# First layer of a two-layer diffusion trunk: row dot products write partial sums, the sink becomes a softmax column, the gate exponentials take their offset as a bias

## The chip, the cores and the metric

The kernel runs on one core of a Trainium2 chip. The metric is device time in microseconds (us) of one execution. Three runs of the kernel before gave 2087.85, 2090.25 and 2090.61 us, median 2090.25. One further execution was recorded by the profiler.

## The reference, cut to what matters

Two layers over 640 tokens (128 context, 512 latent) of width 2048, all in fp32. Every layer first makes its modulation vectors (shift, scale, gate) from a conditioning vector, one set for the context tokens and one for the latent ones:

```
shift, scale, gate = split(silu(cond) @ ada_w[l] + ada_b[l], 3)
h = rms_norm(x, norm_g[l]) * (1 + scale) + shift
y = mixer(h @ w_in) * silu(h @ w_gate);  x = x + gate * (y @ w_out[l])
```

Layer 0 mixes with window attention (8 heads, a sink logit per head that enters the softmax denominator and nothing else) and with gated linear attention (GLA, 4 heads, forward and backward). Of the softmax: `p = softmax([scores, sink])`, then the sink's column is dropped. Of GLA, with `b` the running sum of the log gates inside a 128-token chunk, the elementwise part is

```
Qp = q * exp(b/16)             KS = k * exp((b[end] - b)/16)
QI = q * exp((b - b[mid])/16)  KI = k * exp((b[mid] - b)/16)
```

for both directions and each of five chunks. Layer 1 has neighbourhood attention and a spatial-gating MLP; the change is not about it.

## The kernel before, in words

**The matrix work.** Every projection is `chunk` by `chunk`: 128 output columns, 16 input blocks k of 128 rows, the 640 tokens in two halves of 320 (322 where two shift columns ride along). To keep fp32 accuracy each operand is split into a high and a low part in a format TensorE takes at full speed, and three products are added: `acth*whi`, `actl*whi`, `acth*wlo` (method `mm_k`, issued from `mm`, line 400). Four blocks k make a unit of weights: ScalarE (ACT) rounds the raw weights into `whi`, GpSimd (POOL) subtracts into `wlo`. A unit feeds 24 matmuls. The split weights live in a ring of `RING = 2560` columns (line 39), five units of 512 columns.

**Who fixes the order.** The program is one list per engine, written out when it is built. A planner (`Pace`, with fixed costs by engine and size) keeps a clock for every engine; small jobs are Python generators that are advanced between matmuls (`tick`) and that wait (`until`) till the planner holds their inputs for ready. So what the generators issue, and between which matmuls, follows from the planner's costs, while on the chip each engine runs its list in order and waits on semaphores. All vector, scalar and pool instructions are recorded by one helper, so they all carry line 215; TensorE's matmuls carry line 400, its transposes line 405, and a group of small matmuls at the start line 1432.

**PSUM.** Eight banks. In layer 0 after the start, three serve the projections (`npj = 3`, line 2628), three the small matmuls (`sm`), and banks 6 and 7 (printed bank_73 and bank_74) hold two rows of the conditioning vector, repeated on all partitions.

**The start** (`start`, up to about 150 us) makes layer 0's scale by small matmuls (line 1432) and half of its shift by dot products, and runs the first six chunks in windows as the activations come in. The dot products (`shifts`, line 1455; for later vectors `ada_task`, line 1269) take a row block of 512 weights per instruction: DVE multiplies by the conditioning row and reduces; the sum over the four blocks q of a row is made by passing the accumulator on, as the scalar that the next reduction starts from. Each reduction is two instructions, the product (`CUSTOM_DVE_ANT_0` in the profile, `ISA` in a listing) and a read of the accumulator. When POOL is free by the planner, a dot product for the latent tokens goes there instead (`offload`): POOL multiplies into `prod`, ACT copies `prod` with an accumulator output into a column of `psum`, and four adds fold the four blocks into the result. At the end of the start the shift `sh` is folded, the shift columns of the activations are written, and TensorE transposes `sh` (line 405) before the first chunk that uses shift columns, the 96-wide `w_rb`.

**GLA** (four heads, about 150 to 500 us): for each head the chunks k, q and two of v are projected. The evacuation of a chunk (`lin`) is: DVE multiplies a bank by `rstd`; ACT copies two bias columns of the same bank to `bc`; ACT adds the bias in two pieces. `gla_dir` does the elementwise part for one direction: DVE subtracts `b` from its chunk ends into KS and from its middles into KI over all 640 columns, ACT takes four exponentials of 640 columns, DVE multiplies by q or k. `tok_major` transposes a finished v chunk (five transposes in two small banks, two copies by ACT), and `gla_pe` then begins with the transposes of KS.

**Attention** (to about 830 us) works on pieces of 128 to 512 scores: `soft1` masks and takes the row maximum on DVE, ACT exponentiates with `-max` as bias and an accumulator output `den`; ACT also makes `es = exp(sink - max)`; `soft2` adds `es` to `den` on ACT, DVE takes the reciprocal, ACT scales the piece.

## Time and profile before

| | |
|---|---|
| runs | 2087.85, 2090.25, 2090.61 us; median 2090.25 |
| the profiled execution | 2094.82 us, of which the span from first to last instruction is 2093.0 us |
| granted TensorE clock | 0.996 over the span |
| PE busy | 2047.3 us, 98% of the span |
| DVE, ACT, POOL busy | 1327.3, 1064.4, 1275.1 us |

The engines are PE (TensorE matmul), PEld (its weight load), DVE (VectorE), ACT (ScalarE), POOL (GpSimd), SP (issues DMAs). In a row of the trace, `bank<-ident,arena` means: written tile, then the tiles read; `x4` is the number of instructions; what stands in brackets at the end is the engine's idle time just before and what ended it. Matmuls overlap, so a matmul of 310 ns is followed by the next after about 147 ns, and the idle time that the trace gives for PE is a little less than what a stall costs.

### The profile page before, as it was taken

How to read it: one execution, taken by the hardware profiler on the slowest of the kernel's cores; microseconds unless marked ns; L12 is line 12 of the kernel's file. 1: busy time of each engine (PE TensorE's matmuls, PEld its weight loads, DVE VectorE, ACT ScalarE, POOL GpSimd, SP SyncE). 2: the span in 40 equal slices, each digit the busy share in tenths (PEclk: the TensorE clock that was granted, in tenths of full speed). 3: DMA queues.
4: the chain of work that ended last, by engine and by line, in shares of the span. 5: the costliest groups of instructions: out<-in, count | busy, mean ns of one | idle time of the engine just before them, and what ended most of it. 6: DMA issues, size and time to landing. Idle time of an engine off the chain costs nothing. (4 is left out here: it accounts for less than half of the span.)

```text
span 2093.0 us, 40200 instructions
## 1 busy us (share of the span) xinstructions
PE 2047.3 (98%) x14345; PEld 1995.9 (95%) x14345; DVE 1327.3 (63%) x3070; ACT 1064.4 (51%) x2446; POOL 1275.1 (61%) x1072
## 2 busy tenths in 40 slices
PE   7999999999999999999999999999999999999997
PEld 6889999999999999999999999999999999999997
DVE  4757677676555655788786878787454554456444
ACT  5545555445665765444564434444444554454443
POOL 4655454445545554788765666655555577768884
PEclk9999999999999999999999999999999999999998
DMA  9956333436456444577734454454322334363427
GB/s 367 396 195 205 124 122 110 142 112 188 153 170 190 142 137 148 167 222 226 249 131 135 136 159 153 139 156 139 98 86 95 95 129 135 112 235 121 139 90 251
DMA packets 192697, 340.18 MB, mean 163 GB/s; under 512 B 20752, under 2 KB 70000, under 8 KB 192496
## 3 DMA queue, kind: packets, MB, share of 16 engines
q1 hardware_dynamic: 191296, 336.45, 49.7%
q8 instruction: 112, 1.84, 0.4%
q10 hardware_dynamic: 1200, 1.17, 0.2%
q14 instruction: 89, 0.73, 0.1%
HBM read 303.03 MB, written 31.88 MB: 160 GB/s over the span
## 5 line engine op out<-in xcount | busy, mean ns | idle before, releaser
L400 PE MATMUL bank<-acth,whi 128*128 128x320 f32 (+3 forms) x3320 | 1017.7, 317 | 4.7 <-ACT YB L215 1.4
L400 PE MATMUL bank<-acth,wlo 128*128 128x320 f32 (+3 forms) x3320 | 991.7, 310 | 0.9 <-POOL wlo L215 0.9
L400 PE MATMUL bank<-actl,whi 128*128 128x320 f32 (+3 forms) x3320 | 991.5, 310 | 0.0
L215 POOL TENSOR_TENSOR wlo<-wraw,whi 128x512 fp32r<-128x512 f32 (+1 forms) x446 | 568.1, 1285 | 439.1 <-ACT whi L215 368.4
L400 PEld LDWEIGHTS bank<-acth,whi 128*128 128x128 f32 (+1 forms) x3320 | 614.9, 188 | 12.5 <-issue 3.0
L400 PEld LDWEIGHTS bank<-actl,whi 128*128 128x128 f32 (+1 forms) x3320 | 615.5, 188 | 1.7
L400 PEld LDWEIGHTS bank<-acth,wlo 128*128 128x128 f32 (+1 forms) x3320 | 614.1, 188 | 1.9 <-POOL wlo L215 1.9
L215 POOL TENSOR_TENSOR wlo<-rs,whi 128x384 fp32r<-128x384 f32 x370 | 407.9, 1120 | 205.6 <-ACT whi L215 173.2
L215 ACT ACTIVATE whi<-wraw 128x512 fp32r<-128x512 f32 (+1 forms) x456 | 261.3, 588 | 126.7 <-PE bank L400 85.7
L215 ACT ACTIVATE whi<-rs 128x384 fp32r<-128x384 f32 x370 | 184.4, 518 | 83.2 <-PE bank L400 69.1
L400 PE MATMUL bank<-eh,whi 128*128 128x322 f32 (+1 forms) x666 | 208.9, 314 | 1.0 <-ACT whi L215 1.0
L400 PE MATMUL bank<-eh,wlo 128*128 128x322 f32 (+1 forms) x666 | 206.8, 310 | 1.2 <-POOL wlo L215 0.9
L400 PE MATMUL bank<-el,whi 128*128 128x322 f32 (+1 forms) x666 | 206.3, 310 | 0.0
L215 DVE CUSTOM_DVE_ANT_0 adas<-adas,bank,partg 128x256 bf16<-128x256 f32 (+1 forms) x296 | 160.6, 543 | 15.6 <-DMA adas<-ada_g 8.0
L215 DVE TENSOR_TENSOR wraw<-rs 128x768 f32<-128x768 f32 x74 | 98.8, 1335 | 100.7 <-DMA rs<-w_odd 55.4
L215 POOL TENSOR_TENSOR prod<-adas,mixrow 128x512 f32<-128x512 f32 x76 | 99.4, 1317 | 68.5 <-ACT prod L215 47.9
L215 ACT ACTIVATE arena<-arena,bc 128x512 f32<-128x512 f32 (+4 forms) x189 | 97.8, 538 | 78.6 <-DVE arena L215 73.7
L400 PEld LDWEIGHTS bank<-eh,wlo 128*128 128x128 f32 x666 | 125.1, 188 | 2.4 <-POOL wlo L215 2.4
L400 PEld LDWEIGHTS bank<-eh,whi 128*128 128x128 f32 x666 | 125.4, 188 | 1.3 <-ACT whi L215 1.2
L400 PEld LDWEIGHTS bank<-el,whi 128*128 128x128 f32 x666 | 125.4, 188 | 0.0
L215 DVE CUSTOM_DVE_ANT_0 adas<-adas,bank,part 128x512 bf16<-128x512 f32 x150 | 111.6, 744 | 19.6 <-DMA adas<-ada 16.7
L215 DVE TENSOR_TENSOR bank<-bank,sums 128x320 f32<-128x320 f32 (+1 forms) x148 | 70.8, 493 | 82.5 <-PE bank L400 61.3
(226 smaller groups left out, 2458.9 us busy)
## 6 DMA issues: line engine op xcount, KB each, us to landing
wraw<-w_even SPq DMA_DIRECT2D x176, 256.0 KB, 3.4
adas<-ada_g SPq DMA_DIRECT2D x128, 256.0 KB, 3.7
adas<-ada SPq DMA_DIRECT2D x128, 256.0 KB, 3.7
rs<-w_odd SPq DMA_DIRECT2D x50, 384.0 KB, 3.3
wraw<-w_odd SPq DMA_DIRECT2D x74, 256.0 KB, 3.6
wraw<-w_out SPq DMA_DIRECT2D x60, 256.0 KB, 3.9
rs<-w_odd SPq DMA_DIRECT2D x50, 256.0 KB, 3.8
Y<-ada SPq DMA_DIRECT2D x24, 512.0 KB, 7.8
```

The costliest lines, as they stand in the source:

```text
L215: return f(*args, **kw)
L400: self.nc.tensor.matmul(out, lhsT, rhs, start=start, stop=stop, **kw)
```

## The change

Five edits, all in work around layer 0:

- **Partial sums.** Each dot product over 512 columns writes its own cell of `psum`, now `[128, 2, 4, 32]` (token group, block q, row tile), instead of passing an accumulator on; the scalar operand of the reduction is the constant 0. The new `fold_parts` adds the four blocks of both groups in three adds. Two clearings of `psum` go. Jobs with 256 columns keep the old form.
- **Sink.** The piece is one column wider; POOL writes the sink there, and the one exponential of width w+1 with its accumulator gives the whole denominator. `es` and the add on ACT go.
- **Gate exponentials.** DVE no longer subtracts over 640 columns. Three small DVE instructions (128x5) make the offsets, and ACT takes the exponentials for KS, QI and KI chunk by chunk, five instructions of 128 columns each, with the offset as a bias column. Qp keeps one instruction of 640.
- **Bias columns.** While three banks serve the projections, `bc` is copied out of the bank by DVE, right behind its multiplication, instead of by ACT.
- **Room.** `wg` shares the buffer of `so`; `cols` is new; the pieces have 516 columns instead of 512.

Instructions in the built program: DVE 3072 to 3063, ACT 2278 to 2283, POOL 1074 to 1135, PE 13435 both times. Dot products that go to POOL and ACT: 97 before, 122 now.

```diff
-        self.psum = self.P([128, 4, 32], "psum")
+        self.psum = self.P([128, 2, 4, 32], "psum")
...
-                nc.scalar.activation(bc[:M], pa[:M, 0:2], AF.Copy, scale=scale)
+                if self.npj == 3:
+                    nc.vector.tensor_scalar(bc[:M], pa[:M, 0:2], scale, None, ALU.mult)
+                else:
+                    nc.scalar.activation(bc[:M], pa[:M, 0:2], AF.Copy, scale=scale)
...
-                    acc = self.part[name][:, f + k, c : c + 1]
+                    acc = self.part[name][:, f + k, c : c + 1] if m > 1 else self.psum[:, c, q, f : f + 1]
...
-                        acc if (f + k, c) in begun else 0.0, ALU.mult, ALU.add, acc
+                        acc if m > 1 and (f + k, c) in begun else 0.0, ALU.mult, ALU.add, acc
...
-                    for q in range(4):
-                        acc = self.part[name][:, :, 1]
-                        nc.vector.tensor_tensor(acc, acc, self.psum[:, q, 0 : acc.shape[1]], ALU.add)
-                        if name == "1":
-                            yield 2.0
+                    self.fold_parts(self.part[name].rearrange("p f c -> p c f"))
...
+    def fold_parts(self, out):
+        n = out.shape[2]
+        x = [self.psum[:, :, q, 0:n] for q in range(4)]
+        self.nc.vector.tensor_tensor(x[0], x[0], x[1], ALU.add)
+        self.nc.vector.tensor_tensor(x[2], x[2], x[3], ALU.add)
+        self.nc.vector.tensor_tensor(out, x[0], x[2], ALU.add)
...
-                        nc.vector.tensor_tensor_reduce(
-                            junk, raw, p, 1.0, acc if (f, c) in begun else 0.0, ALU.mult, ALU.add, acc
-                        )
+                        nc.vector.tensor_tensor_reduce(junk, raw, p, 1.0, 0.0, ALU.mult, ALU.add, acc)
...
-        self.act(p[:, :w], p[:, :w], AF.Exp, bias=nm, accum_out=den)
-        es = None
         if sinkcol is not None:
-            es = self.s("es")
-            self.act(es, nm, AF.Exp, bias=sinkcol)
-        return p[:, :w], den, es
+            nc.gpsimd.tensor_scalar(p[:, w : w + 1], sinkcol, 1.0, None, ALU.mult)
+        n = w + (sinkcol is not None)
+        self.act(p[:, :n], p[:, :n], AF.Exp, bias=nm, accum_out=den)
+        return p[:, :w], den, n > w
...
-        if es is not None:
-            nc.scalar.activation(den, es, AF.Identity, bias=den)
...
+        cols = L["cols"][dr]
+        for i, (at, by) in enumerate(((end, 1.0), (mid, -1.0), (mid, 1.0))):
+            nc.vector.tensor_scalar(cols[:, i, :], b5[:, :, at], by / 16, None, ALU.mult)
+        self.act(Qp, b128, AF.Exp, scale=1.0 / 16)
         self.act(etot, b5[:, :, end], AF.Exp, scale=1.0 / 16)
-        nc.vector.tensor_tensor(v5(KS), b5[:, :, end : end + 1].to_broadcast([128, 5, 128]), b5, ALU.subtract)
-        self.act(Qp, b128, AF.Exp, scale=1.0 / 16)
-        nc.vector.tensor_tensor(v5(KI), b5, b5[:, :, mid : mid + 1].to_broadcast([128, 5, 128]), ALU.subtract)
-        yield from self.until(KS, Qp)
-        self.act(KS, KS, AF.Exp, scale=1.0 / 16)
+
+        def exps(x, i, by):
+            for j in range(5):
+                self.act(v5(x)[:, j, :], b5[:, j, :], AF.Exp, scale=by / 16, bias=cols[:, i, j : j + 1])
+
+        yield
+        exps(KS, 0, -1.0)
...
-        self.act(QI, KI, AF.Exp, scale=1.0 / 16)
-        self.act(KI, KI, AF.Exp, scale=-1.0 / 16)
+        exps(QI, 1, 1.0)
         yield from self.until(QI)
         nc.vector.tensor_tensor(QI, q, QI, ALU.mult)
+        exps(KI, 2, -1.0)
...
-            L["wg"] = self.take(256)
+            L["wg"] = L["so"].list[0]
+            L["cols"] = [self.take(16)[:, :15].rearrange("p (a b) -> p a b", b=5) for _ in range(2)]
```

The change also moves instructions, since the planner's costs follow the new instructions. The first place is TensorE's list at the first GLA head, where `tok_major` transposes the last piece of v (the arena, written into bank_71 and bank_72) and `gla_pe` goes on with KS (again the arena, then Y). Before:

```order
L400 MATMUL bank_69<-acth,wlo 128x320
L405 MATMUL bank_71<-ident,arena_1639 128x128 x4
L405 MATMUL bank_72<-ident,arena_1639 128x128
L405 MATMUL bank_71<-ident,arena_1639 128x128 x4
L405 MATMUL bank_70<-ident,arena_1639 128x128
L405 MATMUL bank_70<-ident,Y 128x128
```

With the change:

```order
L400 MATMUL bank_69<-acth,wlo 128x320
L405 MATMUL bank_71<-ident,arena_1632 128x128 x4
L405 MATMUL bank_72<-ident,arena_1632 128x128
L400 MATMUL bank_69<-acth,whi 128x320
L400 MATMUL bank_69<-actl,whi 128x320
L400 MATMUL bank_69<-acth,wlo 128x320
L400 MATMUL bank_69<-acth,whi 128x320
L400 MATMUL bank_69<-actl,whi 128x320
L400 MATMUL bank_69<-acth,wlo 128x320
L405 MATMUL bank_71<-ident,arena_1632 128x128 x4
L405 MATMUL bank_70<-ident,arena_1632 128x128
L405 MATMUL bank_70<-ident,Y 128x128
```

The sixth transpose writes the bank that the first four wrote. It followed the fifth directly; now six projection matmuls stand between them, and 18, 12 and 18 at the other heads, where none stood either. At the third head, though, the four matmuls of `gla_dir` on `r` and `wgs`, which had six projection matmuls between the second and the third, now follow each other; and at the fourth head the last step over the states has 24 projection matmuls ahead of it where it had six. The second place is ACT's list at the second head, between two rounds of weights (`whi`): Y and arena of 128x640 are whole exponentials, of 128x128 the new ones. Before:

```order
L215 ACTIVATE whi<-wraw 128x512
L215 ACTIVATE arena_1639<-bank_71 128x4x128
L215 ACTIVATE arena_1639<-bank_72 128x128
L215 ACTIVATE Y<-Y 128x640
L215 ACTIVATE Y<-arena_1639 128x640
L215 ACTIVATE arena_1639<-arena_1639 128x640
L215 ACTIVATE wgs_1644<-arena_1639 96x256
L215 ACTIVATE Y<-Y 128x640 x2
L215 ACTIVATE whi<-wraw 128x512 x3
```

With the change:

```order
L215 ACTIVATE whi<-wraw 128x512
L215 ACTIVATE Y<-arena_1632 128x640
L215 ACTIVATE etot_2866<-arena_1632 128x5
L215 ACTIVATE arena_1632<-bank_71 128x4x128
L215 ACTIVATE arena_1632<-bank_72 128x128
L215 ACTIVATE arena_1632<-arena_1632 128x128 x5
L215 ACTIVATE Y<-Y 128x640
L215 ACTIVATE etot_2963<-Y 128x5
L215 ACTIVATE Y<-arena_1632 128x128 x5
L215 ACTIVATE Y<-Y,arena_1632 128x128 x5
L215 ACTIVATE wgs_1637<-arena_1632 96x256
L215 ACTIVATE arena_1632<-arena_1632 128x128 x5
```

Behind the last row come one `prod`, five more exponentials and then the next `whi`; eight instructions stood between the two `whi` before where there are 33 now. The third place is the end of DVE's list in the start, where the four adds of `sh` and `psum` have become three:

```order
L215 ISA adas,psum<-raw_305,bank_70 128x512
L215 ISA psum 128x1
L215 TENSOR_TENSOR YB_103<-YB_103,bank_73 128x320
L215 TENSOR_TENSOR psum<-psum 128x2x8 x2
L215 TENSOR_TENSOR sh_119<-psum 128x2x8
L215 TENSOR_TENSOR sh_119<-sh_119,small 128x8 x2
L1131 TENSOR_TENSOR actl<-sh_119,acth 128x16x2
```

From the second round of `rstd` to this fold eight dot products stand on DVE where there were nine; the ninth went to POOL and ACT.

More of the change, by code (lines that the diff above doesn't have):

```diff
@@ L1315, in ada_task @@
                         load(i + 3)
-                    acc = self.part[name][:, f + k, c : c + 1]
+                    acc = self.part[name][:, f + k, c : c + 1] if m > 1 else self.psum[:, c, q, f : f + 1]
                     self.collect()
-                    if c == m == 1 and self.offload(raw[:, 0, :], self.mixrow[q % 2], self.psum[:, q, f : f + 1]):
+                    if c == m == 1 and self.offload(raw[:, 0, :], self.mixrow[q % 2], self.psum[:, 1, q, f : f + 1]):
                         yield
@@ L1378, in start @@
         self.sh0 = self.P([128, 2, KT], "sh0")
-        for x in (self.sh0, self.psum):
-            nc.gpsimd.memset(x, 0.0)
+        nc.gpsimd.memset(self.sh0, 0.0)
         NB = KT - BOTH
@@ L1464, in shifts @@
                     todo += [(f, d["ada_s0"][f, :, cs]) for f in range(NB)]
-                begun = set()
                 def load(i):
@@ L1489, in shifts @@
                             load(i + len(raws) - 1)
-                        acc = self.sh0[:, c, f : f + 1]
+                        acc = self.psum[:, c, q, f : f + 1]
                         self.collect()
-                        if c and self.offload(raw, self.mixrow[q % 2], self.psum[:, q, f : f + 1]):
+                        if c and self.offload(raw, self.mixrow[q % 2], self.psum[:, 1, q, f : f + 1]):
                             yield
                             continue
-                        nc.vector.tensor_tensor_reduce(
-                            junk, raw, p, 1.0, acc if (f, c) in begun else 0.0, ALU.mult, ALU.add, acc
-                        )
-                        begun.add((f, c))
+                        nc.vector.tensor_tensor_reduce(junk, raw, p, 1.0, 0.0, ALU.mult, ALU.add, acc)
                         yield self.pace0
@@ L1502, in shifts @@
                     yield
-                for q in range(4):
-                    x = self.sh0[:, 1, 0:NB]
-                    nc.vector.tensor_tensor(x, x, self.psum[:, q, 0:NB], ALU.add)
+                self.fold_parts(self.sh0[:, :, 0:NB])
                 for c in range(2):
@@ L2247, in open_gla @@
         def open_gla():
-            self.arena(17.2)
+            self.arena(16.86)
             self.rp = tc.tile_pool(name="rp", bufs=1)
@@ L2348, in open_att @@
             self.ckT, self.cv = (self.take(256).rearrange("p (a b) -> p a b", b=128) for _ in range(2))
-            self.pieces = list(self.take(512, 4).list)
+            self.pieces = list(self.take(516, 4).list)
             self.pT = self.take(2048)
```

14 lines of the change are left out of this document (8 added, 6 removed).

## The prediction

> **What bounds the kernel now.** I read the page's busy times first, then a table by stretch, then what TensorE waited for in the stretches that have idle time.
>
> ```profile
> span 2093.0 us, 40200 instructions
> PE 2047.3 (98%) x14345; PEld 1995.9 (95%) x14345; DVE 1327.3 (63%) x3070; ACT 1064.4 (51%) x2446; POOL 1275.1 (61%) x1072
> ```
>
> TensorE is the bound: it has work during 2047.3 of 2093.0 us, and the change leaves its 13435 instructions as they are. So the change can take at most a share of 45.7 us of idle time, and whatever it adds to DVE, ACT or POOL costs nothing until TensorE waits for it. Where the idle time lies (columns: stretch, its length, then busy us of PE, PEld, DVE, ACT, POOL):
>
> ```profile
> 0.00:150.00 150.00, 131.38 (x1420) 117.38 (x1421) 90.58 (x187) 77.79 (x178) 89.89 (x82) 0.99 0.89 327
> 205.00:500.00 295.00, 289.91 (x1986) 283.19 (x1985) 207.45 (x373) 156.35 (x315) 140.22 (x98) 1.00 0.41 126
> 500.00:560.00 60.00, 55.54 (x378) 54.38 (x377) 38.80 (x98) 31.39 (x83) 36.89 (x29) 1.00 0.60 189
> 560.00:830.00 270.00, 269.67 (x1789) 258.74 (x1789) 152.13 (x442) 174.72 (x461) 135.22 (x103) 1.00 0.49 154
> ```
>
> The start has 18.6 us, GLA 5.1, the passage to attention 4.5, attention 0.3. The granted clock in these rows is 0.99 to 1.00, so the clock has nothing to give. The waits of PE from 200 to 500 us (total, times, longest):
>
> ```profile
> PE bank L405 <- ACT arena L215: 3.1, 6, 0.6
> PE bank L400 <- DVE arena L215: 1.8, 4, 0.8
> ```
>
> These the change can reach: the transposes in GLA and the steps over the states; and, at the end of the start, one wait for DVE.
>
> **The start: dot products and fold.** What ends last there is a chain on DVE, while TensorE stands ready:
>
> ```profile
> 146.25 0.28 PE L405 MATMUL bank<-ident,sh 128*32 128x128 f32 x1 [1.14 <-DVE sh L215]
> ...
> 142.71 0.74 DVE L215 CUSTOM_DVE_ANT_0 adas<-raw,bank,sh 128x512 bf16<-128x512 f32 x1
> 143.50 0.69 DVE L215 CUSTOM_DVE_ANT_0 adas<-raw,bank 128x512 bf16<-128x512 f32 x1
> 144.30 1.70 DVE L215 TENSOR_TENSOR sh<-sh,psum 128x8 f32<-128x8 f32 x4
> 145.91 0.29 DVE L215 TENSOR_TENSOR sh<-sh,small 128x8 f32<-128x8 f32 x2
> 144.29 1.01 POOL L215 TENSOR_TENSOR wlo<-wraw,whi 128x384 fp32r<-128x384 f32 x1 [1.30 <-PE bank L400]
> L215 DVE CUSTOM_DVE_ANT_0 adas<-raw,bank,sh 128x512 bf16<-128x512 f32 x28 | 20.9, 746 | 12.2 <-DMA raw<-ada_s 10.2 <-ACT mixrow L215 1.4
> L215 DVE CUSTOM_DVE_ANT_0 adas<-raw,bank 128x512 bf16<-128x512 f32 x15 | 10.2, 680 | 0.5
> ```
>
> A dot product that takes over an accumulator lasts 746 ns, one that starts at a constant 680. Of the last nine, two started at a constant; the change has eight, all of that kind: one step of 0.79 us less (142.71 to 143.50) and six times 0.066, together 1.2 us. The fold took 1.61 us (144.30 to 145.91) for four adds; two adds of the same size take 0.29, so three cost between 0.45 and 1.2 (three quarters of what four took). That is another 0.4 to 1.2 us, and DVE would be 1.6 to 2.4 us earlier. PE can win only the 1.14 us that it stood idle before 146.25: **-1.1 us**, bounds -1.4 (with the work behind it) and 0 (if the ninth product, which goes to POOL and ACT, lands late). [...]
>
> **GLA: the moved transposes.** Here an idle time stands at all four heads in the same place:
>
> ```profile
> 222.68 0.66 PE L405 MATMUL bank<-ident,arena 128*128 128x128 f32 x4 [0.36 <-ACT arena L215]
> 223.91 0.77 PE L405 MATMUL bank<-ident,arena 128*128 128x128 f32 x5 [0.58 <-ACT arena L215]
> ...
> 297.62 0.66 PE L405 MATMUL bank<-ident,arena 128*128 128x128 f32 x4 [0.44 <-ACT arena L215]
> 298.86 0.77 PE L405 MATMUL bank<-ident,arena 128*128 128x128 f32 x5 [0.58 <-ACT arena L215]
> ...
> 372.92 0.77 PE L405 MATMUL bank<-ident,arena 128*128 128x128 f32 x5 [0.58 <-ACT arena L215]
> ...
> 445.87 0.77 PE L405 MATMUL bank<-ident,arena 128*128 128x128 f32 x5 [0.58 <-ACT arena L215]
> ```
>
> The second group of five (KS) waits until ACT has copied the first group out of the bank. In the changed order 6, 18, 12 and 18 projection matmuls stand between the groups. Their step is
>
> ```profile
> 296.47 0.31 PE L400 MATMUL bank<-acth,whi 128*128 128x320 f32 x1
> 296.62 0.31 PE L400 MATMUL bank<-actl,whi 128*128 128x320 f32 x1
> ```
>
> 0.15 us, so even six of them are 0.9 us of work where 0.58 was idle: **-2.3 us** (4 x 0.58), bounds 0 and -3.1 (with the 0.36 and 0.44 that the first groups of two heads waited for their evacuation). The fourth head's last step over the states gets 24 matmuls (3.6 us) ahead of it instead of six; one of the four waits that make 1.8 us goes: **-0.4**. Against it, at the third head four matmuls on `r` and `wgs` follow each other on three small banks. The same group elsewhere:
>
> ```profile
> 269.62 0.52 ACT L215 ACTIVATE arena<-bank,small 128x320 f32<-128x320 f32 x1
> 269.75 1.01 DVE L215 TENSOR_SCALAR Y<-bank,small 128x320 f32<-128x320 f32 x2 [1.91 <-ACT arena L215]
> 270.03 0.74 PE L400 MATMUL bank<-r,wgs 96*128 96x320 f32 x2
> ```
>
> The fourth needs the first's bank, which ACT (0.52) and DVE (0.5) empty one after the other: about 1.4 us after the first began, where its turn comes after 0.6 (three steps of 0.2). **+0.7**, bounds 0 and +1.2.
>
> **The exponentials themselves.** Rows of ACT's timeline:
>
> ```profile
> 280.28 0.40 ACT L215 ACTIVATE arena<-arena,bc 128x128 f32<-128x128 f32 x1
> 280.59 0.19 ACT L215 ACTIVATE etot<-arena 128x5 f32<-128x5 f32 x1
> ...
> 282.68 0.72 ACT L215 ACTIVATE Y<-Y 128x640 f32<-128x640 f32 x1
> 283.30 0.72 ACT L215 ACTIVATE arena<-arena 128x640 f32<-128x640 f32 x1
> L215 DVE TENSOR_TENSOR arena<-arena 128x640 f32<-128x640 f32 x28 | 30.6, 1105 | 0.7 <-ACT arena L215 0.4
> L215 DVE TENSOR_SCALAR nm<-mx 128x1 f32<-128x1 f32 x40 | 6.1, 154 | 1.4
> ```
>
> One of 128 columns with a bias holds ACT for 0.31 us (280.28 to 280.59), one of 640 for 0.62. Per head 30 short ones (9.3 us) replace six long ones (3.7): +5.6 us on ACT. DVE loses four subtractions of about 1.1 us and gets six tiny instructions of about 0.15: -3.5 us. ACT works 156 of 295 us here, so the 22 us for four heads fit; what hides them is TensorE's matmuls on weights already split. That cover is the third rival. I take **0**, bounds 0 and +2 per head.
>
> `wg` in the buffer of `so` adds one wait in each direction, a load for a state store and a state copy for the reading of `wg`; in the order half a head lies between them, so 0.
>
> **What lies beside the path.** Rows for the rest:
>
> ```profile
> 220.84 0.17 ACT L215 ACTIVATE bc<-bank 128x2 f32<-128x2 f32 x1 [4.21 <-DVE arena L215]
> ...
> L215 DVE TENSOR_SCALAR sh<-bank,small 128x2 f32<-128x2 f32 x8 | 1.7, 218 | 6.1 <-PE bank L400 6.1
> L215 ACT ACTIVATE den<-es,den 128x1 f32<-128x1 f32 x40 | 11.5, 286 | 0.0
> L215 ACT ACTIVATE es<-nm,small 128x1 f32<-128x1 f32 x40 | 11.2, 279 | 0.0
> L215 ACT ACTIVATE whi<-wraw 128x512 fp32r<-128x512 f32 x304 | 186.9, 623 | 112.7 <-PE bank L400 76.1 <-issue 10.6 <-POOL wlo L215 9.8
> ```
>
> 37 `bc` copies move from ACT (0.17 us) to DVE (about 0.22): a bank is free about as late as before, 0 with bounds of 0.3 either way. The sink saves ACT 22.7 us in attention and a link of each piece's chain, but TensorE is idle for 0.3 us of those 270: at most -0.3; POOL gets 40 tiny instructions, and the exponential behind each may wait for one POOL instruction (1.01 us at 144.29), which again only costs when the weights run short: +1 at worst, 0 taken. The other dot products give DVE some 15 us, and 25 more of them go to POOL and ACT: TensorE did not wait for either there. In the passage to attention a transposition of v stands idle longer than anything in GLA:
>
> ```profile
> 520.66 0.66 PE L405 MATMUL bank<-ident,arena 128*128 128x128 f32 x4 [1.76 <-ACT arena L215]
> ...
> 518.70 0.75 DVE L215 CUSTOM_DVE_ANT_0 adas<-adas,bank,partg 128x512 bf16<-128x512 f32 x1 [0.64 <-DMA adas<-ada_g]
> ```
>
> The evacuation that it needs stood behind this dot product on DVE, which waited for its DMA. Whether a dot product stands there again, and late, hangs on the order and on DMA: bounds -1.2 (0.64 and half a product) and 0; I take 0.
>
> **Sum:** -1.1 - 2.3 - 0.4 + 0.7 = -3.1 us. The profiled execution, 2094.82 us with 1.8 us around its span, would become 2091.7; it lies 4.6 us above the median of the runs, 2090.25, from which I forecast **2087.1**.
>
> **Rivals.** *More goes than the counted waits.* With DVE relieved and the order looser, the first groups' 0.36 and 0.44, two more waits of the states (0.9) and the 1.2 of the passage go too: another -2.9, **2084.2**. For it speaks that all hang on DVE or ACT being late; against it that their places in the order stay.
>
> *The waits only move.* ACT's copies of the transposed v now queue among weight roundings (0.62 us); two ahead of them use up the 0.9 us, the four waits stay, and -1.1 and +0.7 remain: **2089.8**.
>
> *ACT starves TensorE.* Place: the GLA heads, of which the second has 33 ACT instructions between two roundings of weights: 25 short exponentials of 0.31, two long ones of 0.62 and six others of about 2 us together, 11 us without any wait. The ring holds five units of 24 matmuls, four of them ahead of the one in use: 4 x 24 x 0.15 = 14.4 us. It decides from 3 us of waiting on ACT in that stretch, and a single wait of ACT for DVE can be longer than that (4.21 us before the `bc` of 220.84). If each head lost 2 us, +8 - 3.1 gives +4.9: **2095.2**. Against it: no row of GLA shows TensorE waiting for weights. [...]
>
> **How the numbers follow.** The forecast has 0.48 (its own range 2084.5 to 2089), more gain 0.24, moved waits 0.15, starving 0.13. A difference under 0.2%, 4.2 us, is none for this kernel. Below 2086.1 lie 0.3 of the forecast (0.15) and nearly all of the first rival (0.22): faster 0.37. Slower comes from the third, 0.12; the rest, 0.51, is no difference. Range **2082 to 2093**: it leaves out the starving case and the end of the first rival.
>
> **What would show it.** Right: no idle time before the transpose of `sh`; none before the KS transposes at four heads, about 0.7 us at the third head's `wgs` group; dot products of 512 columns at 680 ns; GLA's idle time 2 us lower; attention unchanged. Wrong: PE rows waiting for `whi` or `wlo` between 200 and 500 us, an idle time that turns up at the next matmul instead, or ACT busy over 200 us there.

## The result and the profile after

The changed kernel takes **2102.86 us** (median of 6 runs, 2098.47 to 2105.61), the kernel before 2090.43 beside it: ratio 1.0058, 95% interval 1.0044 to 1.0073. It is 12.4 us slower, where 3.1 us less was forecast. The profiled execution took 2105.61 us, 10.8 more than the one before; it is the slowest of the six, so its waits are rather at the upper end.

First the page and the table by stretch (columns as before: stretch, its length, busy us of PE, PEld, DVE, ACT, POOL with counts, granted clock, DMA share, GB/s).

```profile
span 2103.8 us, 40382 instructions
PE 2052.8 (98%) x14345; PEld 2003.0 (95%) x14345; DVE 1280.5 (61%) x3061; ACT 1074.8 (51%) x2476; POOL 1313.3 (62%) x1133
...
0.00:150.00 150.00, 134.49 (x1443) 120.74 (x1444) 90.24 (x185) 79.64 (x181) 91.43 (x83) 0.99 0.89 331
205.00:500.00 295.00, 292.01 (x2010) 286.60 (x2009) 192.32 (x404) 175.22 (x408) 148.42 (x106) 1.00 0.42 133
500.00:560.00 60.00, 53.16 (x344) 51.95 (x342) 32.51 (x83) 27.18 (x66) 38.19 (x32) 0.93 0.50 160
560.00:830.00 270.00, 262.65 (x1696) 250.23 (x1697) 153.62 (x481) 161.74 (x397) 156.06 (x150) 0.98 0.53 167
```

The start and GLA are better, as forecast: 15.5 us of TensorE idle time in place of 18.6, and 3.0 in place of 5.1. The loss is in the two rows that I had left out of the sum. Between 500 and 830 us TensorE ran 2040 matmuls (344 + 1696) where it had run 2167 (378 + 1789): 127 fewer (a few records may be missing from either trace), which at the 0.147 us of a projection step is, by estimate, 18.7 us of work not done there. Two things make it up. Idle time rose from 4.8 us (60 - 55.54 and 270 - 269.67) to 14.2, and the granted clock, 1.00 in both rows before, is now 0.93 and 0.98.

What TensorE waited for between 500 and 720 us, before and then after (total, times, longest):

```profile
PE bank L400 <- DVE arena L215: 2.2, 1, 2.2
PE bank L405 <- ACT arena L215: 2.1, 2, 1.8
```

```profile
PE bank L405 <- ACT arena L215: 8.8, 5, 4.1
PE bank L400 <- DVE arena L215: 5.2, 2, 2.8
```

Neither `whi` nor `wlo` appears: TensorE is not short of weights. It waits for roped operands (DVE) and for scaled score pieces that it is to transpose (ACT). Four long waits make most of it; the timeline of TensorE, with the last projection step ahead of the first wait and two steps behind it:

```profile
536.03 0.30 PE L400 MATMUL bank<-acth,wlo 128*128 128x322 f32 x1
539.11 0.80 PE L400 MATMUL bank<-arena 128*128 128x128 f32 x2 [2.78 <-DVE arena L215]
...
541.10 0.47 PE L400 MATMUL bank<-acth,wlo 128*128 128x322 f32 x1
541.37 0.47 PE L400 MATMUL bank<-acth,whi 128*128 128x322 f32 x1
...
560.36 1.11 PE L405 MATMUL bank<-ident,arena 128*128 128x128 f32 x4 [4.08 <-ACT arena L215]
...
637.99 0.90 PE L405 MATMUL bank<-ident,arena 128*128 128x128 f32 x3 [3.21 <-ACT arena L215]
...
688.67 1.65 PE L400 MATMUL bank<-arena 128*128 128x128 f32 x4 [2.47 <-DVE arena L215]
```

Behind the first wait a projection step takes 0.27 us (541.10 to 541.37) in place of 0.15: the clock is at half. The clock record of the trace has such half-clock stretches at 538.4 (6.8 us long), 558.9 (6.8), 637.4, 688.6 and 859.3 us (3.4 each): one at the end of each of these waits, and one behind a wait of 2.6 us that ends at 857.7, in the next stretch. A second profile of the changed kernel (run 9 below) has the last three of the four waits again, 3.98, 2.94 and 2.52 us, each with 3.4 us of half clock; at the first place it has 1.17 and 0.67 us at full clock. The kernel before has none between 51 and 2081 us.

Why TensorE waits at 539.11, in the rows of SyncE's queue and of DVE:

```profile
531.05 0.51 SPq L436 DMA_DIRECT2D Y<-arena  x1
```

```profile
535.48 0.69 DVE L215 TENSOR_TENSOR arena<-arena 128x512 f32<-128x512 f32 x1 [2.73 <-DMA Y<-arena]
537.33 1.73 DVE L215 TENSOR_TENSOR arena<-arena,Y 128x512 f32<-128x512 f32 x1 [1.16 <-POOL Y L215]
```

These are the steps of `rope`. The last of its four swaps is issued at 531.05 and DVE's multiplication starts 4.4 us later; DVE stands still for 2.73 us of it. Then the addition waits 1.16 us for POOL's product, lasts 1.73, and the scores start at its end. A load of 256 KB was issued between the third swap and the fourth, and the fourth landed 4.2 us after its issue. At 560.36 the same thing hits an innocent neighbour: the reciprocal of a finished piece stands behind both rotary steps of the next head.

```profile
555.90 0.69 DVE L215 TENSOR_TENSOR arena<-arena 128x512 f32<-128x512 f32 x1 [4.38 <-DMA arena<-arena]
557.74 1.74 DVE L215 TENSOR_TENSOR arena<-arena 128x512 f32<-128x512 f32 x1 [1.15 <-POOL arena L215]
559.40 0.15 DVE L215 RECIPROCAL den<-den 128x1 f32<-128x1 f32 x1
```

```profile
559.59 0.72 ACT L215 ACTIVATE arena<-arena,den 128x512 f32<-128x512 f32 x1 [5.57 <-DVE den L215]
```

At 637.99 it is POOL: the exponential waits for the sink's copy, which stands behind two `wlo` products (rows of POOL, then of ACT).

```profile
632.50 2.96 POOL L215 TENSOR_TENSOR wlo<-wraw,whi 128x512 fp32r<-128x512 f32 x2
635.42 0.20 POOL L215 TENSOR_SCALAR arena<-small 128x1 f32<-128x1 f32 x1
```

```profile
635.66 0.62 ACT L215 ACTIVATE arena<-arena,nm 128x385 f32<-128x385 f32 x1 [3.45 <-POOL arena L215]
```

So the trace offers two suspects for one edit: the sink's place on POOL's queue, and the order. The planner writes the order from its costs, and a piece whose sink takes two ACT instructions less counts as ready sooner. I counted in the programs' order how many TensorE instructions stand between the scores of a piece and its first transposition (heads 0 to 3, mean of 20 pieces): 39.5 before, 32.2 in the changed kernel. The difference, some 7 instructions or 1.1 us, is cover that a late swap had before; that it is what decides is argued from the count. The swaps were late before too (DVE waited 7.7 + 8.9 us for them between 500 and 720 us, now 8.6 + 11.5; the last swap of the same rotary step landed 4.3 us after its issue).

The count does not bear on the first of the four waits, where the scores themselves wait for the rotary step. By the programs' order 73 TensorE instructions stand between these swaps and these scores in both kernels, and the kernel before waits there too, at full clock:

```profile
546.71 0.49 PE L400 MATMUL bank<-arena 128*128 128x128 f32 x2 [2.15 <-DVE arena L215]
```

So of the first wait only 0.6 us and the half clock are new; the other three are new whole.

### The profile page after: what moved, and what is told of

Its sections match the earlier page's. It is cut to its first block, busy times and chain, and to the rows that moved or that the text cites. A ratio compares the mean times of both kernels' runs of the same rounds, so it can differ in the third digit from the quotient of the medians.

```text
span 2103.8 us, 40382 instructions
## 1 busy us (share of the span) xinstructions
PE 2052.8 (98%) x14345; PEld 2003.0 (95%) x14345; DVE 1280.5 (61%) x3061; ACT 1074.8 (51%) x2476; POOL 1313.3 (62%) x1133
## 3 DMA queue, kind: packets, MB, share of 16 engines
q10 hardware_dynamic: 1200, 1.17, 0.2%
## 4 chain that ended last, share of the span: by engine, by line
PE 62%; issue 1%; DVE 1%; ACT 0%; POOL 0%; DMA 0%; SPq 0%; DVEq 0%; POOLq 0%; ACTq 0%
PE bank L400 61%; PE bank L405 1%; POOL wlo L215 0%; DMA arena<-yT_dram 0%; DVE arena L215 0%; DVE Y L215 0%; ACT arena L215 0%; ACT rstd L215 0%; ACT whi L215 0%; DVE bank L215 0%; DVE rs L215 0%; DVE wlo L215 0%; ACT Y L215 0%; DVE adas L215 0%; ACT eh L215 0%
## 5 line engine op out<-in xcount | busy, mean ns | idle before, releaser
L215 DVE CUSTOM_DVE_ANT_0 adas<-adas,bank 128x512 bf16<-128x512 f32 (+1 forms) x364 | 240.4, 660 | 61.4 <-DMA adas<-ada 25.9
L215 POOL TENSOR_TENSOR prod<-adas,mixrow 128x512 f32<-128x512 f32 x100 | 131.1, 1321 | 88.4 <-ACT prod L215 57.9
L215 DVE CUSTOM_DVE_ANT_0 adas<-adas,bank,partg 128x256 bf16<-128x256 f32 x224 | 107.1, 478 | 6.0 <-ACT bank L215 0.9
```

The costliest lines, as they stand in the source:

```text
L215: return f(*args, **kw)
```

## The experiments

Twelve runs in three groups of four (1 to 4, 5 to 8, 9 to 12), each group on one chip with runs of before among them (medians of before 2090.05, 2088.41 and 2088.54 us), so the ratios are what compares across groups.

| kernel | median us | ratio to before, 95% |
|---|---|---|
| 1 sink put back | 2090.86 | 1.0001 (0.9991 to 1.0011) |
| 2 old order, new sink (POOL) | 2088.97 | 0.9990 (0.9979 to 1.0001) |
| 3 new order, old sink (ACT) | 2101.13 | 1.0048 (1.0031 to 1.0064) |
| 4 new order, sink's copy on DVE | 2095.02 | 1.0023 (1.0011 to 1.0035) |
| 5 throwaway matmuls in the waits | 2099.36 | 1.0056 (1.0044 to 1.0069) |
| 6 rotary step planned 3 us later | 2084.75 | 0.9986 (0.9978 to 0.9995) |
| 7 sink put back, rotary step later | 2083.26 | 0.9977 (0.9967 to 0.9987) |
| 8 before, rotary step later | 2089.77 | 1.0012 (1.0002 to 1.0022) |
| 9 the changed kernel again | 2100.45 | 1.0062 (1.0048 to 1.0075) |
| 10 throwaway matmuls again | 2097.78 | 1.0044 (1.0031 to 1.0058) |
| 11 as 6, exponentials of GLA as before | 2090.69 | 1.0005 (0.9995 to 1.0014) |
| 12 as 6, sink's copy on DVE | 2081.90 | 0.9967 (0.9954 to 0.9979) |

### Order or POOL: runs 1 to 4

The planner can be told one thing while another is emitted: its record of an instruction is a call of its own. So order and sink can be varied apart. Run 1 puts the sink back and lets the order follow.

```
-            nc.gpsimd.tensor_scalar(p[:, w : w + 1], sinkcol, 1.0, None, ALU.mult)
-        n = w + (sinkcol is not None)
-        self.act(p[:, :n], p[:, :n], AF.Exp, bias=nm, accum_out=den)
+        self.act(p[:, :w], p[:, :w], AF.Exp, bias=nm, accum_out=den)
+            es = self.s("es")
+            self.act(es, nm, AF.Exp, bias=sinkcol)
...
+            nc.scalar.activation(den, es, AF.Identity, bias=den)
```

> The changed kernel with the sink alone put back: two small ACT instructions per piece (`es`, then `den`) instead of the POOL copy into the piece, and the order worked out anew for it. If the sink edit is what costs (by its order or by its place on POOL), the TensorE stalls of the changed kernel between 530 and 700 us (2.9, 4.2, 3.4 and 2.6 us, each with half clock behind it) are gone, TensorE's busy time per 25 us there is back to before's, and the start and GLA keep the 3 us they have gained: 2085 to 2090 us. If other edits cost (dot products that moved to POOL and ACT, DVE's `bc`), the stalls stay and the time is 2098 to 2106.

Measured: 2090.86 us, no difference from before. The loss goes with the sink edit, and the dot products, the exponentials and `bc` are cleared of it. The 3 us did not show in the median, though the idle time of GLA in its profile is 3.0 us as in the changed kernel: the first of the four waits, expected to go, is still there, 2.9 us up to 541.75 with 6.8 us of half clock from 541.0 on, where the kernel before has 2.2 us at full clock. It may have taken the 3 us back.

Run 2 holds that order and emits the POOL copy; the planner is told of `es` and `den`.

```
+        real.gpsimd.tensor_scalar(p[:, w : w + 1], sinkcol, 1.0, None, ALU.mult)
+        rec("a", "activation", (p[:, :w], p[:, :w], AF.Exp), dict(bias=nm, accum_out=den))
+        real.scalar.activation(p[:, : w + 1], p[:, : w + 1], AF.Exp, bias=nm, accum_out=den)
+        rec("a", "activation", (es, nm, AF.Exp), dict(bias=sinkcol))
```

> The order of the kernel with the sink put back, held fixed on TensorE, DVE, SyncE and, but for the sink's own instructions, ACT and POOL; in this order the sink is the POOL copy of the changed kernel. If the loss is in the order (each piece counted as ready sooner, so that the TensorE work that needs it stands earlier, with less other work ahead of it), this is as fast as the kernel with the sink put back, 2085 to 2091 us, with no stall over 2.5 us in attention. If the loss is the wait of the exponential for POOL's queue, it stays: ACT waits 15 us or more for the POOL copies in attention, stalls of 3 us stand behind some of them, 2096 to 2106 us.

Measured: 2088.97 us. Its waits of ACT between 500 and 720 us have the POOL copies in them, and its TensorE waits there are those of one swap:

```profile
ACT arena L1653 <- POOL arena L1650: 10.0, 9, 2.0
```

```profile
PE bank L400 <- DVE arena L215: 3.7, 2, 3.4
PE bank L405 <- ACT arena L215: 0.2, 1, 0.2
```

Ten microseconds of waiting for POOL, and next to nothing of it reaches TensorE there. Further on, before 730.96, one exponential waits 6.4 us for its copy, and TensorE 1.2 us for what hangs on it; the time shows nothing of either. The wait of 3.4 us, with 3.4 us of half clock, is again the first of the four; a stall over 2.5 us had not been expected here. Run 3 is the opposite corner: the changed kernel's order, with `es` and `den` on ACT and no copy on POOL.

```
+        rec("g", "tensor_scalar", (p[:, w : w + 1], sinkcol, 1.0, None, ALU.mult), {})
+        rec("a", "activation", (p[:, :n], p[:, :n], AF.Exp), dict(bias=nm, accum_out=den))
+        real.scalar.activation(p[:, :w], p[:, :w], AF.Exp, bias=nm, accum_out=den)
+        real.scalar.activation(es, nm, AF.Exp, bias=sinkcol)
```

> The other corner: the order of the changed kernel, held fixed, with the two small ACT instructions per piece in the place of the POOL copy. Order theory: the stalls at 536, 556 and 686 us, which stand behind the swaps of the rotary step and DVE's queue, stay with their half clock; 2097 to 2105 us. POOL theory: no wait for POOL is left, so 2086 to 2092 us.

Measured: 2101.13 us, ratio 1.0048, with no POOL copy in the program at all. Its TensorE waits between 500 and 720 us:

```profile
PE bank L405 <- ACT arena L215: 8.1, 5, 3.7
PE bank L400 <- DVE arena L215: 2.7, 2, 1.5
```

In its profile (2097.28 us, the fastest of its six runs) only the wait before 556 is as long as in the changed kernel and has half clock behind it; at 536 and 680 us two waits of 1.2 to 1.7 us stand in place of one long one, so the expected half clock came at one place of three.

The four corners are thus 1.0001 and 0.9990 in the old order, 1.0048 and about 1.006 in the new one: with the same instructions the order makes 0.5 to 0.7%, and within one order POOL's copy differs from `es` and `den` by 0.1% either way. The POOL theory, that without POOL's copy there is no loss, falls. Run 4 still has something to say for POOL's part.

```
-            nc.gpsimd.tensor_scalar(p[:, w : w + 1], sinkcol, 1.0, None, ALU.mult)
+            x = (p[:, w : w + 1], sinkcol, 1.0, None, ALU.mult)
+            self.pace.record("g", "tensor_scalar", x, {})
+            self.tc.nc.vector.tensor_scalar(*x)
```

> The changed kernel in its own order; only the engine of the 40 copies into the piece is another, DVE instead of POOL (each about 0.2 us, right behind `nm` on DVE's queue). The waits of ACT for POOL's copies (22.8 us, 12 times, in 500 to 720 us) go. Order theory: of TensorE's stalls only the one at 634 us (3.4 us, and about 1.5 us of half clock) and the 0.8 us at 691 can go, the others stay: about 2099 us, between 2096 and 2103. POOL theory: 2087 to 2092 us.

Measured: 2095.02 us, just under what the order theory gave and above what the POOL theory gave. In this order, which has little slack, a wait for POOL does cost (0.35 to 0.4% against the changed kernel), but so do `es` and `den` in run 3. Order and instructions thus do not simply add: the new order costs 0.23% with the copy on DVE, 0.48% with `es` and `den`, and about 0.6% with the copy on POOL. The old order with the copy on DVE was not run, and why `es` and `den` cost 0.25% more than the copy on DVE is not shown. What remains with the copy on DVE I put down to the swaps: its profile keeps 10.8 us of waits for DVE and ACT between 500 and 720 us, the longest of 3.0 and 3.9 us, at the changed kernel's first two places.

### The swaps: runs 6 to 8

One line in `rope`, which makes the planner count the swapped rows as landing 3 us later:

```
         yield from self.until(sw)
+        yield 3.0
         nc.vector.tensor_tensor(q[:, s], q[:, s], self.cos, ALU.mult)
```

> The changed kernel with one line more: in the rotary step the order is made as if the swapped rows landed 3 us later, so that the two multiplications and all that hangs on them are put later on DVE, POOL, ACT and TensorE. If the stalls come from swaps that land later than the order counts on (4.4 us from the issue of the last one in the profile), DVE no longer waits 3 to 6 us for them, the stalls at 536, 556 and 686 us shrink below 1.5 us without half clock behind them, and the time is 2085 to 2093. If the whole chain only moves 3 us later and stalls there as before, 2099 to 2106.

Measured: 2084.75 us, ratio 0.9986, 0.7% less than the changed kernel. Rows of its SyncE queue and of DVE at the first rotary step, and the table by stretch:

```profile
529.70 0.51 SPq L436 DMA_DIRECT2D Y<-arena  x1
```

```profile
532.86 0.69 DVE L215 CUSTOM_DVE_ANT_0 adas<-adas,bank 128x512 bf16<-128x512 f32 x1 [2.62 <-DMA adas<-ada]
533.47 1.44 DVE L215 TENSOR_TENSOR arena<-arena 128x512 f32<-128x512 f32 x1
535.02 1.58 DVE L215 TENSOR_TENSOR arena<-arena,Y 128x512 f32<-128x512 f32 x1
```

```profile
205.00:500.00 295.00, 292.00 (x2009) 286.60 (x2009) 192.43 (x405) 176.07 (x410) 148.71 (x106) 1.00 0.43 133
500.00:560.00 60.00, 59.38 (x399) 57.58 (x398) 39.45 (x111) 29.73 (x72) 40.01 (x37) 1.00 0.65 202
560.00:830.00 270.00, 268.00 (x1782) 257.78 (x1781) 164.41 (x515) 164.09 (x391) 147.70 (x143) 1.00 0.56 178
```

A dot product that DVE needs anyway now stands ahead of the rotary step, and the multiplication, 3.8 us after the issue of the last swap, finds its rows landed. Between 500 and 720 us DVE waits for swaps 2.3 us in all (20.1 in the changed kernel); idle time from 500 to 830 us is 2.6 us in place of 14.2, at full clock. The pieces stand as near their transpositions as in the changed kernel (31.3 instructions on the mean, after 32.2), so short cover alone does not make the loss. That it does so together with a late swap is what these runs speak for; the line moves other instructions too, the dot products among them.

> The kernel with the sink put back (2090.9 us) with the same line in the rotary step. It has one stall behind a swap in its profile (3.1 us at 538 us, with 6.8 us of half clock behind it). Late swaps: both go, about 5 us, 2084 to 2088. Only moved: 2089 to 2093.

> The kernel before with the same line in the rotary step. Its one stall behind a swap is 2.3 us, at 544 us, without half clock in the profile. Late swaps: 1.5 to 2.5 us less than before's 2090, at most 4 where other executions fall to half clock there. Only moved: within 1.5 us of before.

Measured: 2083.26 us for the kernel with the sink put back, a gain of 0.24% on run 1; 2089.77 us for the kernel before, ratio 1.0012, no gain and perhaps a small loss. For the kernel before I had expected 1.5 to 2.5 us less. Its profile has 1.9 us less idle time between 500 and 560 us, but the median does not show it: its swaps were covered but for one wait, and there is little for the line to win.

Run 7's swap stall did not go altogether: in its profile (2088.83 us, the slowest of its runs) the last swap of the first step lands 4.8 us after its issue, TensorE waits 2.2 us at the first of the four places, and half clock follows.

Runs 6, 7 and 8 have the line in common, and so price the edits in orders that allow for the swaps. Against run 8 the edits without the sink are worth 0.35% (run 7, 0.9977 to 1.0012), with it 0.26% (run 6). The sink edit itself gains nothing there: 0.1% the other way, within the intervals.

### The parts that were to gain: runs 11 and 12

Run 11 takes run 6 and puts back the exponentials of GLA (per head four subtractions on DVE, and long exponentials).

```
-        exps(KS, 0, -1.0)
+        nc.vector.tensor_tensor(v5(KS), b5[:, :, end : end + 1].to_broadcast([128, 5, 128]), b5, ALU.subtract)
...
+        self.act(KS, KS, AF.Exp, scale=1.0 / 16)
```

> The kernel with the later rotary step (2084.75 us), with the gate exponentials of GLA as before (four subtractions on DVE, long exponentials). If it is the exponentials that took the 2.1 us of idle time out of GLA, the idle time of 205 to 500 us is back from 3.0 to about 5.1 us and the time 2 us higher, 2086 to 2088. If the order in GLA comes from another part, it stays at 3.0 and the time within 1 us of 2084.75.

```profile
205.00:500.00 295.00, 287.56 (x1970) 280.52 (x1968) 204.60 (x392) 155.43 (x309) 150.31 (x104) 1.00 0.41 130
```

Measured: 2090.69 us, 0.19% above run 6, and 7.4 us of idle time in GLA where run 6 has 3.0. The exponentials are what took the idle time out of GLA; in this order they are worth 4.4 us of it rather than 2.1, so the time, too, came out above the 2086 to 2088 expected. The waits of transposes for ACT are back with 4.6 us, which none of the other kernels with the new exponentials has. (The profile is of the fastest of its runs, 2085.65 us.)

Run 12 takes run 6 and gives the sink's copy to DVE, planned as such:

```
-            nc.gpsimd.tensor_scalar(p[:, w : w + 1], sinkcol, 1.0, None, ALU.mult)
+            nc.vector.tensor_scalar(p[:, w : w + 1], sinkcol, 1.0, None, ALU.mult)
```

> The kernel with the later rotary step, with the sink's copy given to DVE instead of POOL, in an order made for that. If POOL's queue still holds exponentials back there, 1 to 3 us less than 2084.75; if the later swaps have already given the exponentials the time that POOL's copy needs, within 1 us of it.

Measured: **2081.90 us**, ratio 0.9967 (0.9954 to 0.9979), 0.19% below run 6 and the fastest of all: faster than both kernels. The idle time from 560 to 830 us is 0.7 us where run 6 has 2.0. That is not yet the whole difference, the two orders are not the same, and the intervals of runs 6 and 12, on two chips, just meet; so the 0.19% is no clean price of POOL's queue in run 6.

```profile
560.00:830.00 270.00, 269.27 (x1795) 259.71 (x1794) 161.56 (x520) 168.90 (x397) 146.56 (x113) 1.00 0.55 175
```

### The half clock: runs 5, 9 and 10

Ten throwaway matmuls ahead of the waiting instruction at each of the four places:

```
+        def warm(out):
+            for _ in range(10):
+                self.tc.nc.tensor.matmul(out, self.ident, self.ident, start=True, stop=True)
...
+            if (h, t) in ((0, 1), (4, 1)):
+                warm(ps[:, 0:128])
...
+            if (h, t) in ((0, 3), (3, 4)):
+                warm(pt[:, 0:128])
```

> The changed kernel in its own order; only, at the four places where its TensorE stood idle for 2.6 to 4.2 us (536, 556, 634 and 686 us), ten throwaway matmuls of the identity by itself (20 passes of 0.11 us, 2.2 us) stand just ahead of the waiting instruction, into the bank that it then overwrites. They can't end a wait, so if the idle times alone make the loss the time stays at 2100 to 2106. If a good part of the loss is the half clock that follows a long idle time (6.8, 6.8, 3.4 and 3.4 us at granted clock 0.5 in the profile, some 17.5 us of them with work, so 8.7 us lost), the granted clock stays at 1.0 from 530 to 700 us and the time falls to about 2094, between 2091 and 2097.

```profile
538.50 2.39 PE L1699 MATMUL bank<-ident 128*128 128x128 f32 x20
542.09 0.49 PE L400 MATMUL bank<-arena 128*128 128x128 f32 x2 [1.20 <-DVE arena L215]
...
500.00:560.00 60.00, 57.45 (x400) 56.36 (x399) 32.40 (x82) 28.29 (x68) 38.75 (x33) 1.00 0.54 170
```

The granted clock stayed at 1.00 from 530 to 700 us, as it should. The time hardly followed: 2099.36 us, just under the 2100 to 2106 of a loss by idle time alone, ratio 1.0056 where the changed kernel had 1.0058. So both were run side by side.

> The changed kernel once more, beside the next one on the same chip: 0.45 to 0.7% over before, so about 2099 to 2103 where before has 2089; mean granted clock 0.991 to 0.994.

> The kernel with the throwaway matmuls at four idle places once more, beside the changed kernel. The profile of its first run had no half clock between 530 and 700 us and was 6.2 us shorter than the changed kernel's profile, but its median over before was the same (0.56 against 0.58%). If half clock behind a long idle time costs what its length says, it is 3 to 7 us below the changed kernel; if the engines that TensorE waits for set the pace anyway, so that a slower TensorE only waits less, the two agree within 1.5 us.

Measured: 2100.45 and 2097.78 us, 2.7 apart, between the two expectations, with overlapping intervals (1.0048 to 1.0075 and 1.0031 to 1.0058). Over both pairs the throwaway matmuls are worth some 2 us, not the 8.7 that I had worked out from the length of the half clock, and zero is not excluded. At the first place of run 5 the throwaway work and the wait that is left take 3.6 us together (538.50 to 542.09), where the changed kernel lost 3.1 (536.03 to 539.11), so part of what a full clock saves may be waited for again; that is argued, not shown. That half clock follows these waits is shown; what it costs here stays open between 0 and about 4 us.

## Why the prediction was wrong

**The step that failed** is the sink in "What lies beside the path": "The sink saves ACT 22.7 us in attention and a link of each piece's chain, but TensorE is idle for 0.3 us of those 270: at most -0.3 ... +1 at worst, 0 taken". It costed the edit in the order of before. But a shorter chain off the critical path goes to the planner, which spends it on putting scores and transpositions closer (39.5 instructions to 32.2), and with that goes cover against late swaps (4.4 us from issue to use at the first rotary step). The reason given for 0, that a wait behind POOL "again only costs when the weights run short", failed as well: TensorE's long waits in attention are for score pieces and roped operands, none for weights. The same line holds what should have warned: 0.3 us idle says that everything was covered, not by how much. "Attention unchanged", which was to show the forecast right, is where it broke. The +12.4 us hang on the order: with the sink's instructions held, it makes 0.5 to 0.7% (runs 1 to 3 and the changed kernel), and run 6, which keeps the sink edit and plans the rotary step for swaps that land later, has 0.9986. Which part of the new order costs how much is not separated: the first rotary step has the same place in both, and the copy's engine decides over half of the price (run 4).

**POOL's part** was named (an exponential that waits for one POOL instruction, +1), too small: the wait at 635.66 is 3.45 us, behind two `wlo` products. It decides nothing in the old order (run 2); with short cover and later swaps it costs some 0.19% by the medians (run 6 against run 12, not clear of the noise), and in the changed kernel's own order 0.35 to 0.4% (run 4), some 4 and 8 us.

**The start, -1.1: right.** Rows of DVE, then of TensorE:

```profile
142.10 0.25 DVE L215 TENSOR_TENSOR psum<-psum 128x16 f32<-128x16 f32 x2
142.39 0.17 DVE L215 TENSOR_TENSOR sh<-psum 128x16 f32<-128x16 f32 x1
142.60 0.24 DVE L215 TENSOR_TENSOR sh<-sh,small 128x8 f32<-128x8 f32 x2
```

```profile
143.04 0.27 PE L405 MATMUL bank<-ident,sh 128*32 128x128 f32 x1
```

The fold takes 0.50 us (142.10 to 142.60; 0.45 to 1.2 was forecast), the dot products 684 ns on the mean (680 forecast), and no wait is left before the transposition of `sh`. Run 8, which has the old start, has that wait again, 1.0 us. The idle time of the whole start fell by more, 3.1 us, but that is not the edit's: it is 15.0 to 17.6 us in the profiles of the other kernels with the edit, and 16.3 in run 8 without it. Beside the old fold POOL worked for 1.01 us (144.29), beside the new one it ran two memsets (141.90, 0.80 us); how much of the 1.1 us that the fold is shorter is the adds' own is not shown.

**GLA, -2.3 - 0.4 + 0.7 = -2.0: the sum right, measured -2.1, by other terms.** (Timeline of TensorE at the second and third head, then its waits from 200 to 500 us):

```profile
294.55 0.71 PE L405 MATMUL bank<-ident,arena 128*128 128x128 f32 x5
297.76 0.71 PE L405 MATMUL bank<-ident,arena 128*128 128x128 f32 x5
...
340.46 0.41 PE L400 MATMUL bank<-r,wgs 96*128 96x320 f32 x1 [0.92 <-DVE Y L215]
```

```profile
PE bank L400 <- DVE arena L215: 1.4, 4, 0.4
PE bank L400 <- DVE Y L215: 0.9, 1, 0.9
PE bank L400 <- DVE bc L215: 0.6, 1, 0.6
```

No transposition waits for ACT any more, at none of the four heads: -3.1, the far bound, since the first groups' 0.36 and 0.44 went too. The waits of the states fell by 0.4, as forecast. The `wgs` group costs 0.9 (0.7 forecast; the working, 1.4 less 0.6, gives 0.8), and a wait of 0.6 for a `bc` copy on DVE is new, where 0.3 was the bound.

**The exponentials, 0: right.** Five of them hold ACT for 1.57 us, 0.31 each, and ACT works 175 us of GLA, under the 200 that I had named; TensorE waits for no weights there. The third rival (ACT starves TensorE) fails.

```profile
280.18 1.57 ACT L215 ACTIVATE arena<-arena 128x128 f32<-128x128 f32 x5
```

**The passage, 0 within -1.2 and 0: past the better end in the counted wait, wrong for the stretch.** The transposition of v that waited 1.76 us waits 0.33 (at 512.37), a gain of 1.4 us. (The bound was added up wrongly: 0.64 and half a product of 0.75 make 1.0.) The stretch of 500 to 560 us as a whole lost, with 6.8 us of idle time for 4.5, by the two waits behind the swaps.

**`wg` in the buffer of `so` and the other dot products: 0, not contradicted.** Run 1 has both and is level with before. Run 6, with all edits in and the line in `rope`, comes to 3.7 us below before; that this is about the forecast's 3.1 is luck, since its order is another.

So the sum's terms held as idle time in the profiles, and parts of the first rival came too (the first groups, the passage). No rival foresaw the loss: they looked for trouble where the edits add work, and none in a stage whose chain an edit had only shortened.

## What to carry to other kernels

Where a planner writes the order, an edit that shortens a chain off the critical path is not free: count in the new order how many instructions now stand between producer and consumer on the busy engine, and compare that cover with the real landing times in the trace (here 4.4 us from the issue of a small transfer, behind a load, to its use) before calling it zero. A stage that shows 0.3 us of idle time may be just covered; look at the waits of the *other* engines there: DVE already stood 16.6 us for those swaps between 500 and 720 us. When a change fails that way, try the planner's landing time before giving up the edit: with that one line the same edits gain 0.14%, and with the copy on DVE's queue 0.33%. Then ask what the edit is still worth: with the line and the old sink the gain is 0.23% (run 7), so no run shows a gain of the sink edit clear of the noise.

## What the runs showed of the hardware

Behind the start, every TensorE wait of 2.2 us or more in the fourteen profiles (2.20 to 4.08 us) came with 3.4 or 6.8 us of half clock, which began between 1.5 us before its end and 1.6 us behind it; a projection step then took 0.27 us in place of 0.15. A little lower it went both ways: not in the kernel before (2.15 us, up to 546.7) nor in run 9 (2.02 us, up to 852.6), but in run 7 (1.96 us, up to 838.0, half clock from 838.2 on); what decides there is not shown. In the changed kernel the five stretches from 538.4 on begin 20.48, 78.51, 51.20 and 170.67 us apart, 6, 23, 15 and 50 times 3.413 us, which is the length that the clock record gives for the shorter ones (6.827 for the longer). Half clock came behind rows of shorter waits too: run 6 has it from 879.1 us on, behind waits of 0.7, 1.2 and 0.5 us that end at 872.6, 877.7 and 878.8, and run 3 from 891.7 on, behind 0.95 and 0.53 us; the kernel before has 0.95 and 0.52 us at the same place as run 3 without it.

The split operands show their worth in time as well: a projection matmul of 320 columns takes its turn every 0.147 us, 0.46 ns a column, where ten plain fp32 matmuls of 128x128 took 2.39 us in run 5 (20 rows of the trace at 538.50), 1.87 ns a column. At these two widths three split products cost 1.38 ns a column.

Two elementwise instructions on two operands, one on POOL and one on DVE, that start together were not both slowed in these profiles: the one that started first kept its time. So it is in all 29 such pairs of 128x512 that start within 0.15 us of each other between 500 and 830 us in the two profiles: about 1.75 us in place of 0.69 on DVE, or about 1.8 in place of 1.3 on POOL. The two pairs whose starts agree to 0.01 us went one each way. In the changed kernel DVE's first rotary multiplication takes 0.69 us and POOL's 1.81 (both start at 535.48); in the kernel before POOL's takes 1.29 and DVE's 1.83 (543.15 and 543.16). The wait for POOL of the addition behind them went with it: 1.16 us in the changed kernel, nothing in the kernel before.

```profile
535.48 1.81 POOL L215 TENSOR_TENSOR Y<-Y,arena 128x512 f32<-128x512 f32 x1 [2.43 <-PE bank L400]
```

```profile
543.15 1.29 POOL L215 TENSOR_TENSOR Y<-Y,arena 128x512 f32<-128x512 f32 x1 [2.38 <-DMA Y<-arena]
```

```profile
543.16 1.83 DVE L215 TENSOR_TENSOR arena<-arena 128x512 f32<-128x512 f32 x1 [4.48 <-DMA Y<-arena]
```
